# Plain and seven-product column pairs by block, and operand sums made in the output projection

## Chip, core and metric

One core of one Trainium2 chip runs one program. The time is the device time in microseconds (us); the kernel before was timed in three runs. The engines are named as in the profile: PE (TensorE, matmuls), DVE (VectorE), ACT (ScalarE), POOL (GpSimd), SP (the queue that starts most transfers). The metric is the time of the whole program, in which three feed-forward layers are the parts that the change touches.

## What is computed

Two transformer blocks over 512 tokens of width 1024, in float32. The parts around the change are three gated feed-forward layers, two in the first block (one at its start, one at its end) and one in the second:

```python
def swiglu(h, w1, w3, w2):
    return (jax.nn.silu(h @ w1) * (h @ w3)) @ w2

# first block, D_FF = 2816
x = x + 0.5 * swiglu(rms_norm(x, norm_ffn1[l]), ffn1_w1[l], ffn1_w3[l], ffn1_w2[l])
x = x + hybrid_mixer(...)
x = x + memory_attention(...)
x = x + 0.5 * swiglu(rms_norm(x, norm_ffn2[l]), ffn2_w1[l], ffn2_w3[l], ffn2_w2[l])
...
# second block, D_FF_2 = 2816
gate, up = gu[..., :D_FF_2], gu[..., D_FF_2:]
x = x + rmsnorm((jax.nn.silu(gate) * up) @ w_ffn_down[l], g_post_ffn[l])
```

Below, block 1, 2 and 3 are these three feed-forward layers in the order in which they run.

## The kernel before

Every float32 matrix is split into a high and a low part in the fast float32 form (the cast at L93 or L94 on ACT, the subtraction at L98 or L99 on DVE), and each product is three matmuls at L109: high x high, high x low, low x high. The tokens lie along the columns, 512 in all, the features along the 128 partitions.

The up stage of a feed-forward layer (`UpPairs`) makes the 22 column tiles of 128 features of both weights, "gate" and "up", in 11 pairs n = 0 to 10. A pair goes in one of two ways. A *plain* pair multiplies tile "a" and tile "b" of both weights with all 512 tokens: 2 tiles x 2 weights x 8 row tiles x 3 matmuls of 512 columns. A *seven-product* pair treats the two column tiles, the two halves of the tokens and the even and odd row tiles as 2 x 2 blocks and makes seven block products instead of eight, each of 2 weights x 4 row tiles x 3 matmuls of 256 columns. Their left operands are pieces and sums of weight tiles: f1 (products 1 and 2), s12 (6 and 5), s34 (7 and 3) and a22 (4); the sums are made on DVE at L213 and L214 (for s12) and L216 and L217 (for s34) and then split. Their right operands are pieces of x (b11 for 1, b21 for 2, b22 for 3) and sums of pieces of x (t2 for 6, t1 for 5, t3 for 7, t4 for 4). These *operand sums* are made once a layer by `Operands.sums`, for each of the four pairs of row tiles: two scaled copies on ACT (L379, L380), three small operations on DVE (L382, L383, L384), and a split (L93 on ACT, L98 on DVE). The products of a pair accumulate in three PSUM banks x, y and z; between them ACT copies bank x (L464), and DVE adds and multiplies out (L472 to L513).

`up_steps` writes the order out by hand: for a seven-product pair 1, then products 4 and 3 of the pair before it, then 2, 6, 5, 7. `PLAIN = (0, 1)` makes the first two pairs of each of the three layers plain. In block 1 `first` runs the four products of pair 0 row tile by row tile, while x comes in; in block 2 only the two of its tile "a", while the last tiles of the output projection (`out_proj` with "mo") still come out at L2041. After `first`, `sums` makes the operand sums for all four row pairs. The norm's sums over the features (8 small matmuls), the root on POOL (L325), a diagonal matrix (L332), 8 matmuls that broadcast it, and the copy to rb (L337) come behind the next plain product; outputs wait for rb. POOL squares and adds x for the norm of block 2 (L296, L300).

Weight tiles come in the order of `Stream.order`: a transfer of 512 KB into one of 6 raw buffers (L166, on SP), the weight sums two entries ahead, the split, and `next`, which works 4 entries ahead. Results of splits, operand sums, weight sums, x and the attention output all lie in one pool of 39 buffers of 4 KB a partition ("q"); temporaries lie in a pool of 8 ("b"). A planner orders each engine's instructions before the program runs; the order of the program text is its priority, and it takes later instructions forward where it expects an engine to be idle.

The functions, as they stand before:

Of the kernel before, what the change touches and what calls it, by code (L numbers as in the profile page):

```python
# [15 lines left out]
P = 128  # L16
# [3 lines left out]
KD = D // P  # L20
# [329 lines left out]
class Operands:  # L350
# [11 lines left out]
    def add(self, x1, x2, g1, g2, c=slice(0, S), pin=None):  # L362

        k = self.k
        if c.start == 0:
            self.b1.append(k.q([P, 2, S], F32R))
            self.b2.append(k.q([P, 2, S], F32R))
            self.x.append((x1, x2, g1, g2))
        j = next(j for j in range(KD // 2) if self.x[j][0] is x1)
        k.split(self.b1[j][:, 0, c], self.b1[j][:, 1, c], x1[:, c], g1, pin is not None)  # L370
        if pin is not None:
            pin()
        k.split(self.b2[j][:, 0, c], self.b2[j][:, 1, c], x2[:, c], g2, pin is not None)
# [30 lines left out]

PLAIN = (0, 1)


def up_steps():


    o, prev = [], None
    for n in range(NF // 2):
        rest = [(prev, 4), (prev, 3)] if prev is not None else []
        if n in PLAIN:
            o += [(n, "a")] + rest + [(n, "b")]
        else:
            o += [(n, 1)] + rest + [(n, 2), (n, 6), (n, 5), (n, 7)]
        prev = None if n in PLAIN else n
    return o + ([(prev, 4), (prev, 3)] if prev is not None else [])


class UpPairs:
# [8 lines left out]

    def __init__(self, k, keys, ops, finish, side=2, halves=None):
        self.k, self.keys, self.ops, self.side = k, keys, ops, side
        self.finish, self.halves = finish, halves
        self.w, self.bank, self.c = {}, {}, {}
        self.rb = None
        self.g = [k.half() if n is None else None for n in range(NF)]
# [110 lines left out]
    def run(self):  # L548
        k = self.k
        steps = up_steps()  # L550
        which = {1: "x", 6: "x", 7: "x", 4: "x", 5: "y", 3: "y", 2: "z"}
        done = {"a": "a", "b": "b", 4: "a22", 3: "s34", 5: "s12", 2: "f1"}
        last = None
        pend = []
        ps0 = self.first()
        if self.halves is None:
            self.ops.sums()
        for n, num in steps:
# [16 lines left out]
            if self.rb is None and last is not None:  # L575
                self.rb = last()
            if self.rb is not None:
                while pend:
                    m, ab, ps = pend.pop(0)
                    self.out_plain(2 * m + (ab == "b"), *ps)  # L580
                if (n, 11) in self.c:
                    z = self.c.pop((n, 11))
                    self.out(2 * n, 0, z, z)
# [74 lines left out]

def up_order(W, keys, srcs):
    seen = set()  # L660
    for n in range(NF // 2):
        W.pairs[n, keys] = {}
    for n, num in up_steps():
        what = UpPairs.LEFT[num][0]
# [1236 lines left out]
def tile_block(ctx: ExitStack, tc: tile.TileContext, aps, out):  # L1901
# [9 lines left out]
    def ffn_order(n, gate, up, down):  # L1911
        up_order(W, (gate, up), (aps[gate], aps[up]))
        for f in range(NF // 2):
# [50 lines left out]

    up = UpPairs(k, ("ffn1_w1", "ffn1_w3"), ops, lambda norm=norm: norm.finish(None, k.rb), 4)
    del ops
# [73 lines left out]
    for d, p in out_proj(k, "mo", cat, list(range(KD))):  # L2040
        nc.vector.tensor_add(x[d], p, x[d])  # L2041
        if d % 2 == 1:
            next_pair(x, ops, d - 1, G["norm_ffn2"], norm)
        nc.scalar.dma_start(x3d[d], x[d])
    x.clear()

    up = UpPairs(k, ("ffn2_w1", "ffn2_w3"), ops, lambda norm=norm: norm.finish(None, k.rb))
    del ops
# [17 lines left out]
def second_order(W, a):  # L2066
# [33 lines left out]
    for d in range(KD):  # L2100
        W.add(("wo2", d), a["w_out_2"][d])
    up_order(W, ("gate", "up"), (a["w_ffn_in"][0:NF], a["w_ffn_in"][NF : 2 * NF]))
    for f in range(NF):
# [3 lines left out]
def second_mix(k, G, x, xs, norm, norm5, k2d, v2d, dr, out):  # L2107
# [206 lines left out]

    up = UpPairs(k, ("gate", "up"), ops, finish, 6, lambda: resid(1))
    g = up.run()
# [192 lines left out]
```

## Time and profile before

| | us |
|---|---|
| median of 3 runs | 2210.93 (2210.76 to 2211.31) |
| the profiled execution | 2209.04 |
| its span, from the first to the last instruction | 2207.2 |
| PE busy | 2182.1 (99%) |
| DVE busy | 1518.6 (69%) |
| ACT busy | 1021.0 (46%) |
| POOL busy | 299.0 (14%) |

Times in the rows are from the start of the span. The up stage of block 1 lies at about 6 to 239 us, the output projection ahead of block 2 at about 765 to 804, block 2's up stage at 804 to 1033, and block 3's at 1847 to 2075. A timeline row merges neighbouring instructions of one line; the number behind x is their count, and the bracket names the idle time before them and what ended it. A matmul is drawn longer than its distance to the next one, because matmuls overlap, so the distance is read from a row's length and its count. The share of busy time over the whole span hides stages in which another engine is full; the tables by stage show those.

### The profile page before, as it was taken

The page shows a single profiled execution, that of the slowest core. Times are in us where ns is not written, and L with a number is a line of the kernel's source. Part 1 is how long each engine was busy: PE and PEld are TensorE (multiplying, and loading weights), DVE is VectorE, ACT ScalarE, POOL GpSimd, SP SyncE. Part 2 cuts the span into 40 slices and gives each one's busy share as a digit, 9 for nine tenths or more (in the row PEclk, how much of TensorE's full clock was granted, in tenths as well). Part 3 has the DMA queues.
Part 4 walks back from the last instruction along what each step waited for, and adds up shares of the span by engine and source line. Part 5 has one row for each costly group of instructions (what it writes and reads, how often), then busy time and mean ns, then how long its engine had stood idle before and what let it go on. Part 6 is the DMA issues. An engine that isn't in the chain of part 4 may idle for free.

```text
span 2207.2 us, 32709 instructions
## 1 busy us (share of the span) xinstructions
PE 2182.1 (99%) x12746; PEld 1902.7 (86%) x12746; DVE 1518.6 (69%) x2605; ACT 1021.0 (46%) x1794; POOL 299.0 (14%) x347
## 2 busy tenths in 40 slices
PE   9999999999999999999999999999999999999998
PEld 8999888878888889999888878887787789999987
DVE  7988644656866667888455955736888757888842
ACT  6554523445344544455333543315666636554620
POOL 0000021301234030000140000312334200000000
PEclk9999999999999999999999999999999999999999
DMA  5233524212333332335234123541111353133431
GB/s 177 98 114 115 177 63 136 82 58 86 122 127 105 108 112 77 115 108 178 62 114 152 54 86 101 176 148 59 41 66 53 125 177 115 58 115 106 162 106 39
DMA packets 79652, 235.73 MB, mean 107 GB/s; under 512 B 9092, under 2 KB 13444, under 8 KB 79496
## 3 DMA queue, kind: packets, MB, share of 16 engines
q1 hardware_dynamic: 75032, 226.12, 31.2%
q10 hardware_dynamic: 4464, 7.52, 0.9%
q8 instruction: 100, 1.64, 0.3%
q14 instruction: 56, 0.46, 0.1%
HBM read 216.30 MB, written 17.30 MB: 106 GB/s over the span
## 4 chain that ended last, share of the span: by engine, by line
PE 84%; DVE 8%; ACT 3%; issue 2%; POOL 2%; DMA 1%; SPq 0%; POOLq 0%; DVEq 0%; ACTq 0%
PE ps L109 82%; PE ps L118 2%; DVE q L98 2%; ACT q L93 1%; ACT q L1770 1%; DVE nx L1768 1%; POOL hr L325 1%; DVE q L99 0%; DMA raw<-in_ffn_w_dram 0%; ACT b L285 0%; DVE q L1668 0%; DVE b L289 0%; DVE q L2260 0%; DVE q L1563 0%; POOL q L1601 0%
## 5 line engine op out<-in xcount | busy, mean ns | idle before, releaser
L109 PE MATMUL ps<-q,q 128*128 128x256 f32 (+3 forms) x11736 | 2108.8, 340 | 7.7 <-ACT b L464 3.9
L109 PEld LDWEIGHTS ps<-q,q 128*128 128x128 f32 x11736 | 1794.8, 190 | 240.3 <-issue 6.6
L98 DVE TENSOR_TENSOR q<-raw,q 128x1024 fp32r<-128x1024 f32 (+3 forms) x389 | 429.6, 1122 | 97.5 <-ACT q L93 55.5
L93 ACT CAST q<-raw 128x1024 fp32r<-128x1024 f32 (+3 forms) x389 | 351.0, 931 | 106.9 <-PE ps L109 69.4
L98 DVE TENSOR_TENSOR q<-q,q 128x1024 fp32r<-128x1024 f32 (+1 forms) x188 | 189.7, 1026 | 59.3 <-ACT q L93 51.9
L93 ACT CAST q<-q 128x1024 fp32r<-128x1024 f32 (+1 forms) x188 | 164.6, 893 | 135.5 <-PE ps L109 66.0
L296 POOL TENSOR_TENSOR b<-q 128x512 f32<-128x512 f32 x32 | 36.9, 1156 | 708.4 <-DVE q L1975 301.5
L473 ACT ACTIVATE b<-b 128x256 f32<-128x256 f32 x108 | 44.9, 417 | 138.8 <-DVE b L472 138.8
L1770 ACT ACTIVATE q<-ps,nx 128x128 f32<-128x128 f32 (+3 forms) x128 | 67.4, 531 | 56.7 <-DVE nx L1768 25.8
L1775 POOL TENSOR_SCALAR q<-q,nr 128x128 f32<-128x128 f32 (+3 forms) x128 | 72.1, 569 | 143.5 <-DVE nr L1773 99.7
L118 PE MATMUL ps<-ident,q 128*128 128x128 f32 x512 | 81.3, 274 | 6.2 <-POOL q L1775 2.5
L464 ACT COPY b<-ps 128x512 f32<-128x512 f32 x81 | 47.3, 584 | 83.7 <-PE ps L109 83.7
L118 PEld LDWEIGHTS ps<-ident,q 128*128 128x128 f32 x512 | 61.8, 140 | 24.3 <-POOL q L1775 8.1
L98 DVE TENSOR_TENSOR q<-ps,q 128x512 fp32r<-128x512 f32 x112 | 74.2, 682 | 11.2 <-ACT q L93 10.8
L94 ACT ACTIVATE q<-q,gains 128x512 fp32r<-128x512 f32 (+1 forms) x48 | 30.5, 648 | 105.2 <-DVE q L1975 34.6
L300 POOL TENSOR_TENSOR b<-b,b 128x512 f32<-128x512 f32 (+1 forms) x49 | 70.4, 1444 | 2.8
L93 ACT CAST q<-ps 128x512 fp32r<-128x512 f32 x112 | 62.7, 593 | 16.8 <-PE ps L109 11.7
L1768 DVE TENSOR_REDUCE nx<-ps 128x1 f32<-128x384 f32 (+3 forms) x96 | 56.0, 584 | 0.0
L99 DVE SCALAR_TENSOR_TENSOR q<-q,gains,q 128x512 fp32r<-128x512 f32 (+1 forms) x48 | 35.6, 754 | 19.9 <-ACT q L94 19.1
L325 POOL TENSOR_TENSOR sr<-ss,mhalf 128x4 f32<-128x4 f32 x8 | 8.1, 1008 | 296.5 <-DVE ss L1400 187.3
L474 DVE TENSOR_TENSOR q<-b,b 128x256 f32<-128x256 f32 x81 | 33.8, 421 | 19.2 <-ACT b L473 18.9
L325 POOL TENSOR_TENSOR or<-ov,mhalf 128x1 f32<-128x1 f32 x4 | 2.2, 547 | 324.2 <-DVE ov L2360 324.2
(264 smaller groups left out, 1426.2 us busy)
## 6 DMA issues: line engine op xcount, KB each, us to landing
raw<-in_ffn_w_dram SPq DMA_DIRECT2D x100, 512.0 KB, 4.3
raw<-in_w_ffn_in_dram SPq DMA_DIRECT2D x44, 512.0 KB, 3.7
raw<-in_w_gm_dram SPq DMA_DIRECT2D x24, 512.0 KB, 3.3
raw<-in_ffn_w2a_dram SPq DMA_DIRECT2D x22, 512.0 KB, 4.5
raw<-in_w_ffn_down_dram SPq DMA_DIRECT2D x22, 512.0 KB, 4.4
raw<-in_w_out_dram SPq DMA_DIRECT2D x16, 512.0 KB, 3.3
raw<-in_w_mk_dram SPq DMA_DIRECT2D x8, 512.0 KB, 3.6
raw<-in_w_mv_dram SPq DMA_DIRECT2D x8, 512.0 KB, 4.0
```

Of the source, the lines that this page charges most:

```text
L93: return self.nc.scalar.copy(out, in_)
L98: return self.nc.vector.tensor_sub(out, in_, hi.bitcast(F32))
L99: return self.nc.vector.scalar_tensor_tensor(out, in_, gain, hi.bitcast(F32), op0=ALU.mult, op1=ALU.subtract)
L109: return self.nc.tensor.matmul(out, a, b, start=start, stop=stop, skip_group_check=skip)
L118: return self.nc.tensor.transpose(out, in_, self.ident[:n, :n])
L296: k.nc.gpsimd.tensor_tensor(t, x, x, op=ALU.mult)
L300: k.nc.gpsimd.tensor_tensor(self.acc, self.acc, t, op=ALU.add)
L464: self.k.nc.scalar.copy(z, bank)
L473: nc.scalar.activation(t, t, AF.Silu)
L1768: nc.vector.tensor_reduce(mx, s.rearrange("p j b t -> p b j t"), axis=AX.XY, op=ALU.max, negate=True)
L1770: nc.scalar.activation(pr[b][:, :n], s[:, :, c, :], AF.Exp, bias=mx[:, c : c + 1], accum_out=sm[:, c : c + 1])
L1775: nc.gpsimd.tensor_scalar(pr[b][:, :n], pr[b][:, :n], r[:, c : c + 1], 1.0, op0=ALU.mult, op1=ALU.mult)
```

## The change

`PLAIN` goes; the plain pairs become an argument: pair 0 alone in block 1, none in block 2, pairs 0 and 1 in block 3 as before. In block 1, pair 1 is made by seven products; the norm's sums now follow its product 1. In block 2, where no pair is plain, products 1 and 2 of pair 0 run together, row pair by row pair, in place of the plain products of tile "a", and the norm's sums follow them. The operand sums of block 2 are made in the loop of the output projection, for each row pair as soon as its two tiles of x are there, ahead of the transfer of x to x3d; the index in `Operands.add` is adapted to that, since `sums` empties its list.

```diff
@@ -366,7 +366,7 @@
-        j = next(j for j in range(KD // 2) if self.x[j][0] is x1)
+        j = next(j for j in range(len(self.x)) if self.x[j][0] is x1) + len(self.b1) - len(self.x)
@@ -402,20 +402,17 @@
         return self.th[j][:, i], self.tl[j][:, i]
 
 
-PLAIN = (0, 1)
-
-
-def up_steps():
+def up_steps(plain):
 
 
     o, prev = [], None
     for n in range(NF // 2):
         rest = [(prev, 4), (prev, 3)] if prev is not None else []
-        if n in PLAIN:
+        if n in plain:
             o += [(n, "a")] + rest + [(n, "b")]
         else:
             o += [(n, 1)] + rest + [(n, 2), (n, 6), (n, 5), (n, 7)]
-        prev = None if n in PLAIN else n
+        prev = None if n in plain else n
     return o + ([(prev, 4), (prev, 3)] if prev is not None else [])
@@ -429,8 +426,8 @@
     LEFT = {"a": ("a", 0), "b": ("b", 0), 1: ("f1", 0), 2: ("f1", 1), 3: ("s34", 1), 4: ("a22", 0), 5: ("s12", 0), 6: ("s12", 1), 7: ("s34", 0)}
     RIGHT = {1: "b11", 2: "b21", 3: "b22", 4: "t4", 5: "t1", 6: "t2", 7: "t3"}
 
-    def __init__(self, k, keys, ops, finish, side=2, halves=None):
-        self.k, self.keys, self.ops, self.side = k, keys, ops, side
+    def __init__(self, k, keys, ops, finish, plain, side=2, halves=None):
+        self.k, self.keys, self.ops, self.first_plain, self.side = k, keys, ops, plain, side
         self.finish, self.halves = finish, halves
         self.w, self.bank, self.c = {}, {}, {}
         self.rb = None
@@ -547,14 +544,28 @@
 
     def run(self):
         k = self.k
-        steps = up_steps()
+        steps = up_steps(self.first_plain)
         which = {1: "x", 6: "x", 7: "x", 4: "x", 5: "y", 3: "y", 2: "z"}
         done = {"a": "a", "b": "b", 4: "a22", 3: "s34", 5: "s12", 2: "f1"}
         last = None
         pend = []
-        ps0 = self.first()
-        if self.halves is None:
-            self.ops.sums()
+        if 0 in self.first_plain:
+            ps0 = self.first()
+            if self.halves is None:
+                self.ops.sums()
+        else:
+            ps0 = []
+
+            for w in "xz":
+                self.bank[0, w] = k.ps([P, 2, 256])
+            for j in range(KD // 2):
+                self.product(0, 1, self.bank[0, "x"], True, [j])
+                self.product(0, 2, self.bank[0, "z"], True, [j])
+            self.take(0, 1)
+            self.take(0, 2)
+            last = self.finish()
+            steps = steps[2:]
+            self.w.pop((0, "f1"))
         for n, num in steps:
             if ps0:
                 ps, ps0 = ps0[:2], ps0[2:]
@@ -574,6 +585,8 @@
                 self.take(n, num)
             if self.rb is None and last is not None:
                 self.rb = last()
+            if self.rb is None and num == 1:
+                last = self.finish()
             if self.rb is not None:
                 while pend:
                     m, ab, ps = pend.pop(0)
@@ -656,11 +669,11 @@
     return fill
 
 
-def up_order(W, keys, srcs):
+def up_order(W, keys, srcs, plain):
     seen = set()
     for n in range(NF // 2):
         W.pairs[n, keys] = {}
-    for n, num in up_steps():
+    for n, num in up_steps(plain):
         what = UpPairs.LEFT[num][0]
         if (n, what) in seen:
             continue
@@ -1909,7 +1922,7 @@
     nc.gpsimd.memset(k.mhalf, -0.5)
 
     def ffn_order(n, gate, up, down):
-        up_order(W, (gate, up), (aps[gate], aps[up]))
+        up_order(W, (gate, up), (aps[gate], aps[up]), (0,) if n == 0 else ())
         for f in range(NF // 2):
             W.add((down, "a", f), aps[down + "a"][f])
         for d in range(4, KD):
@@ -1962,7 +1975,7 @@
         norm.add_fast(x[d], True)
     x.clear()
 
-    up = UpPairs(k, ("ffn1_w1", "ffn1_w3"), ops, lambda norm=norm: norm.finish(None, k.rb), 4)
+    up = UpPairs(k, ("ffn1_w1", "ffn1_w3"), ops, lambda norm=norm: norm.finish(None, k.rb), (0,), 4)
     del ops
     g = up.run()
     for d in range(KD):
@@ -2041,10 +2054,11 @@
         nc.vector.tensor_add(x[d], p, x[d])
         if d % 2 == 1:
             next_pair(x, ops, d - 1, G["norm_ffn2"], norm)
+            ops.sums()
         nc.scalar.dma_start(x3d[d], x[d])
     x.clear()
 
-    up = UpPairs(k, ("ffn2_w1", "ffn2_w3"), ops, lambda norm=norm: norm.finish(None, k.rb))
+    up = UpPairs(k, ("ffn2_w1", "ffn2_w3"), ops, lambda norm=norm: norm.finish(None, k.rb), ())
     del ops
     g = up.run()
     for d in range(KD):
@@ -2099,7 +2113,7 @@
         W.add(("proj", 0, d), a["w_proj_nsa"][d])
     for d in range(KD):
         W.add(("wo2", d), a["w_out_2"][d])
-    up_order(W, ("gate", "up"), (a["w_ffn_in"][0:NF], a["w_ffn_in"][NF : 2 * NF]))
+    up_order(W, ("gate", "up"), (a["w_ffn_in"][0:NF], a["w_ffn_in"][NF : 2 * NF]), (0, 1))
     for f in range(NF):
         W.add(("down", f), a["w_ffn_down"][f])
@@ -2312,7 +2326,7 @@
 
         return second
 
-    up = UpPairs(k, ("gate", "up"), ops, finish, 6, lambda: resid(1))
+    up = UpPairs(k, ("gate", "up"), ops, finish, (0, 1), 6, lambda: resid(1))
     g = up.run()
     gb = k.q([P, 2, S])
     nc.sync.dma_start(gb, k.a["g_post_rows"])
```

## Rows read from the trace of the kernel before

**Rows 1.** The page: header, PE, granted clock by slices, the chain that ended last:

```profile
span 2207.2 us, 32709 instructions
...
PE 2182.1 (99%) x12746; PEld 1902.7 (86%) x12746; DVE 1518.6 (69%) x2605; ACT 1021.0 (46%) x1794; POOL 299.0 (14%) x347
...
PEclk9999999999999999999999999999999999999999
...
PE 84%; DVE 8%; ACT 3%; issue 2%; POOL 2%; DMA 1%; SPq 0%; POOLq 0%; DVEq 0%; ACTq 0%
```

**Rows 2.** The table by stage for L109: window, PE busy (count), weight loads, granted clock, DMA:

```profile
core 0: us, PE busy (x) PEld busy (x), PEclk, DMA share, GB/s
70.00:110.00 40.00, 40.00 (x335) 40.00 (x335) 1.00 0.33 107
...
190.00:230.00 40.00, 40.00 (x335) 40.00 (x335) 1.00 0.39 122
...
245.00:280.00 35.00, 35.00 (x156) 28.99 (x155) 1.00 0.44 138
```

**Rows 3.** The timeline of PE at the start of block 1: start, length, engine, line, operation:

```profile
6.37 6.64 PE L109 MATMUL ps<-q,q 128*128 128x512 f32 x25
...
13.30 21.84 PE L109 MATMUL ps<-q,q 128*128 128x512 f32 x95 [0.29 <-DVE q L99]
...
34.97 0.95 PE L109 MATMUL ps<-ones,b 128*128 128x1 f32 x8
...
42.18 22.68 PE L109 MATMUL ps<-q,q 128*128 128x512 f32 x144
...
66.72 43.45 PE L109 MATMUL ps<-q,q 128*128 128x256 f32 x360 [1.86 <-ACT b L464]
```

**Rows 4.** The timeline of DVE there: weight splits, operand sums, then a weight sum:

```profile
24.35 1.22 DVE L98 TENSOR_TENSOR q<-raw,q 128x1024 fp32r<-128x1024 f32 x1
...
29.65 0.42 DVE L382 TENSOR_TENSOR q<-b,b 128x256 f32<-128x256 f32 x1
...
30.56 0.69 DVE L384 TENSOR_TENSOR q<-b,q 128x512 f32<-128x512 f32 x1
...
32.52 1.23 DVE L98 TENSOR_TENSOR q<-q,q 128x1024 fp32r<-128x1024 f32 x1 [1.27 <-ACT q L93]
...
45.03 1.23 DVE L98 TENSOR_TENSOR q<-q,q 128x1024 fp32r<-128x1024 f32 x1 [1.11 <-ACT q L93]
...
46.18 0.68 DVE L213 TENSOR_TENSOR q<-raw 128x512 f32<-128x512 f32 x1
```

**Rows 5.** The timeline of ACT there: an operand sum's cast, then a weight tile's:

```profile
43.96 1.05 ACT L93 CAST q<-q 128x1024 fp32r<-128x1024 f32 x1 [3.75 <-DVE q L384]
44.91 1.05 ACT L93 CAST q<-raw 128x1024 fp32r<-128x1024 f32 x1
```

**Rows 6.** The timeline of SP there: transfers of weight tiles issued:

```profile
17.28 3.41 SPq L166 DMA_DIRECT2D raw<-in_ffn_w_dram  x4
```

**Rows 7.** Tables by stage over all engines: late in block 1, then block 2's output projection:

```profile
core 0: us, PE busy (x) PEld busy (x) DVE busy (x) ACT busy (x) POOL busy (x), PEclk, DMA share, GB/s
190.00:230.00 40.00, 40.00 (x335) 40.00 (x335) 34.28 (x53) 20.24 (x30) 0.00 (x0) 1.00 0.39 122
...
772.00:804.00 32.00, 32.00 (x143) 26.50 (x142) 19.35 (x19) 10.33 (x13) 16.92 (x13) 1.00 0.48 156
```

**Rows 8.** Timelines at the start of block 2: DVE, POOL and ACT:

```profile
803.92 0.69 DVE L2041 TENSOR_TENSOR q<-ps,q 128x512 f32<-128x512 f32 x1 [2.63 <-PE ps L109]
...
805.40 0.93 DVE L99 SCALAR_TENSOR_TENSOR q<-q,gains,q 128x512 fp32r<-128x512 f32 x1 [0.79 <-ACT q L94]
...
805.87 1.62 POOL L300 TENSOR_TENSOR b<-b,b 128x512 f32<-128x512 f32 x1
...
825.13 1.99 ACT L93 CAST q<-raw 128x1024 fp32r<-128x1024 f32 x2
```

## The prediction

> **What bounds the kernel now.** I read the page first. TensorE (PE) is busy for 2182 of 2207 us at full clock, and 84% of the chain that ended last is PE [rows 1]: the time falls only where PE gets less to do, and rises by every us for which PE has to wait. The next view is the table by stage for the matmul line, since the change swaps one kind of product for another. In a stage of seven-product pairs 335 matmuls of 256 columns go in 40.00 us, 119.4 ns each; in a stage of 512 columns 156 go in 35.00 us, 224 ns [rows 2]. Some records may be missing from such a count, so I check it on the first plain pair: 95 matmuls in 21.84 us less the 0.2 us by which the last is drawn out, 228 ns [rows 3]. I take 226 ns. Last come the timelines around the places that change, to see what lies beside PE there: VectorE (DVE) [rows 4], ScalarE (ACT) [rows 5], the transfer queue [rows 6], and DVE's load by stage [rows 7]; for the second block [rows 8].
>
> **The change part by part.** *The matmuls.* A plain pair is 2 tiles x 2 weights x 8 x 3 = 96 matmuls of 512 columns: 96 x 226 ns = 21.7 us. A seven-product pair is 7 x 2 x 4 x 3 = 168 of 256 columns: 168 x 119.4 ns = 20.0 us. Three pairs change kind, so PE loses 3 x 1.7 = 5.1 us of work: 1.7 in block 1, 3.4 in block 2. The transfers stay: four weight tiles for a pair of either kind. The Trainium skill (TensorE: Matmul & The Clock Gate, section "Back-to-back issue gap") gives 2.5 ns over the columns at 2.4 GHz for each matmul, so 109 and 216 ns, a gain of 2.4 us a pair; the measured spacings differ from it, and with its figures the whole sum below would be 2.1 us lower.
>
> *The work beside PE.* A seven-product pair costs DVE 34.28/2 = 17.1 us of each 20 [rows 7]; a plain one costs four splits and four output steps, about 4 x 1.14 + 4 x 0.60 = 7 us by their spacing. So a plain pair is also a cover: 14 us in which DVE can do other things. That is what is taken away.
>
> *Block 1.* Before, PE has issued 25 + 95 = 120 matmuls when the norm sums start at 34.97 us, 24 of them of the second plain pair [rows 3]; pair 0 therefore ends at 34.97 - 24 x 0.226 = 29.5 us. At 29.65 DVE starts the operand sums and ends them at 45.03 + 1.23 = 46.2 us: four steps of 3.9 us, each three small operations, a cast on ACT, and a subtraction that waits for the cast [rows 4]. All that is hidden behind the second plain pair; t2 is wanted first by product 6 of pair 2, after 53 us. Now pair 1 has seven products. Products 1 and 2 (48 matmuls, 5.7 us) need no sums; the norm sums take some 0.8 us of the 0.95 that are drawn, and the broadcast, eight small matmuls too, as much [rows 3]. At 29.5 + 7.3 = 36.8 us product 6 wants t2, and nine matmuls later, at 37.9, its last quarter. Even if the operand sums ended at 46.2 as before, PE would wait.
>
> They end later. In the text the splits of f1 and s12 and the weight sums for s12 and s34 stand ahead of the operand sums. The four splits replace the four of the plain pair; the weight sums are new: 8 operations of 0.68 us, spaced by 0.60 [rows 4], 4.9 us. Could DVE do them in the gaps between the steps? All these results lie in the pool of 39 q buffers, and the trace says that its buffers are given out in the order of the text: the transfers of pair 2's f1 tiles were issued by 20.7 us [rows 6], ACT sat idle for 3.75 us ahead of 43.96, and yet their cast begins at 44.91, behind the last cast of the operand sums, after which it stands in the text [rows 5]. Block 2 shows the same at 825.13 [rows 8]. So I put the 4.9 us ahead of the chain: the sums end at about 51.1 us.
>
> In the meantime PE can do the three quarters of products 6 and 5 whose operands are there, 36 matmuls or 4.3 us if it may run ahead within a bank, 2.1 us if not. The wait is 51.1 - 36.8 - 4.3 = 10.0 us, at most 12.2; with the sums at 46.2 it would be 5.1. Behind product 6 on PE stand products 5 and 7 and the next pair's first; nothing else of the kernel can run there. The splits for product 7 follow the sums on DVE (2.3 us) while PE still has 12 matmuls (1.4 us) and the first half of product 7 needs one split only: 0.2 us more. Against that, the 1.86 us for which PE waited at 66.72 behind a copy on ACT [rows 3] belongs to the old change from plain to seven-product pairs and goes. Block 1: 10.2 - 1.7 - 1.9 = +6.6 us (bounds +1.5 and +8.8).
>
> *Block 2.* The output projection has room: 19.35 of 32.00 us busy on DVE [rows 7], 12.6 free, against three chains of 2.8 us of DVE work and four weight sums (2.4) before the last x. The fourth chain decides. x7 is added at 803.92, its split ends at 806.33 [rows 8]; 1.5 + 1.05 + 1.23 us of sums follow: 810.2. PE starts on products 1 and 2 at 803.9, is through at 809.6, does the norm sums (0.8), and comes to the last quarter of t2 at 811.5. The norm's accumulator is ready at 805.87 + 1.62 = 807.5 on POOL [rows 8], 2 us before PE asks. Before, the cover was two plain pairs; now it is 1.3 us, and each us of DVE work that slips ahead of the fourth chain beyond that is a us of wait. Two splits of s12 may (2.3 us): I set 0.2 us, with bounds 0 and 3.5. The x3d transfers, now behind the sums in ACT's text, cost nothing: they are read again only in the next stage. Block 2: -3.4 + 0.2 = -3.2 us.
>
> Sum: +6.6 - 3.2 = +3.4 us. On the profiled execution (2209.04 us, span 2207.2) that is 2212.4; the median lies 1.89 us above it, so 2214.3 us.
>
> **The rivals.** *A, the forecast* (0.47): as above, 2212.5 to 2217. *B, the wait also costs clock* (0.15, slower): PE never waits longer than 1.9 us today and the granted clock is full throughout [rows 1, 3], so no row shows what a wait of 10 us, in pieces of 3 to 4, does. Were it to fall to 1.2 GHz, the remaining 12 matmuls and the 24 of product 7 would take twice 119 ns: +4.3 us, 2218.6. The Trainium skill (same page, section "HAM oscillation — how this bites in real kernels") says that PE's clock is halved after idle gaps and comes back with activity; no run here shows it yet. *C, block 2 loses its gain* (0.12, slower): near 803 us the q pool would hold x 1, the attention output 8, b 8, t 6, two output weights 4, f1 4, s12 4 and weight sums 4, which is 39, all there are; if s12 and s34 have to wait for the projection's end, their 4.6 us of splits and sums come ahead of the fourth chain, which takes the 3.4 us: 2217.7. It decides from 1.3 us of slip. *D, the gaps are filled* (0.16): if the weight sums go into the 1.1 us in which DVE waits for each cast, the operand sums end at 46.4 and the wait is 5.3: block 1 +1.9, sum -1.3, 2209.6. For it speaks that DVE is idle there; against it rows 4 to 6. *E, all is hidden* (0.10, faster): the planner puts the operand sums ahead of all else and PE waits no longer than the 1.9 us of today: -5.1, 2205.8. The sums would have to be ready by 38 us, 8 earlier than now, with DVE busy without a gap from 24.35 [rows 4].
>
> **How the numbers follow.** The likeliest is A: 2214.3. A measurement can tell about 0.2%, 4.4 us: 2206.5 and 2215.4 are the limits. Faster is E: 0.10. Slower is B, C and the upper fifth of A: 0.15 + 0.12 + 0.10 = 0.37. The rest of A and D is the same: 0.53. The range leaves out E and the far ends of B and C: 2208.5 to 2219.
>
> **What would show it.** In the profile after: PE spacing unchanged; in block 1 an idle PE between 37 and 51 us put down to the subtraction or cast of the operand sums; weight sums ahead of them on DVE; the last sum at about 51 us; a granted clock below 1.00 there if B holds; in block 2 no PE wait over 1 us and the up stage some 3 us shorter. Wrong would be: operand sums in block 1 done by 40 us, or a PE wait around 810.

## The result and the profile after

The kernel after the change takes 2228.81 us (median, 2228.33 to 2229.81), the kernel before, on the same chip, 2211.11: a ratio of 1.0082, 95% interval [1.0071, 1.0093], slower by 17.7 us where +3.4 was forecast. The range ended at 2219.0.

To place the time I use landmarks that both kernels have. Block 2's first addition of a projection output to x (L2041 before, L2054 after) starts at 770.60 us before and at 782.34 after: +11.7, all of block 1. The first matmul of the down projection behind block 2 starts at 1033.05 before and at 1052.44 after: from landmark to landmark 262.45 and 270.10, so block 2 gives +7.7. That sums to 19.4; the two spans (2207.2 and 2226.5) differ by 19.3, so block 3 adds nothing. The medians differ by 1.7 less, because the trace before is of a quick run (2209.04, median 2211.11): twelve traces of this study have block 1 as before, and their first x addition starts at 770.53 to 773.60. So block 1's share is uncertain by some 3 us. Block 2's is firm: four traces with its two plain pairs give 262.45 or 262.46 us.

The page of the kernel after (header, busy time by engine, granted clock by slices), which answers to [rows 1]:

```profile
span 2226.5 us, 33227 instructions
...
PE 2186.7 (98%) x12962; PEld 1916.9 (86%) x12962; DVE 1553.2 (70%) x2662; ACT 1036.5 (47%) x1821; POOL 300.0 (13%) x347
...
PEclk8999999999999999999999999999999999999999
```

PE has less to do (three times 168 matmuls of 256 columns in place of 96 of 512), and yet its busy time has risen by 4.6 us: part of its matmuls ran slower. The first slice of the clock, now 8, says where to look. The timeline of PE at the start of block 1 (start, length, engine, line, operation, count, idle time before and what ended it), for [rows 3]:

```profile
32.63 0.95 PE L109 MATMUL ps<-ones,b 128*128 128x1 f32 x8
33.45 3.11 PE L109 MATMUL ps<-q,q 128*128 128x256 f32 x24
41.95 2.36 PE L109 MATMUL ps<-b,ones 128*128 128x128 f32 x8 [5.39 <-DVE b L332]
43.96 2.74 PE L109 MATMUL ps<-q,q 128*128 128x256 f32 x12
48.38 0.50 PE L109 MATMUL ps<-q,q 128*128 128x256 f32 x2 [1.68 <-ACT q L93]
49.64 1.13 PE L109 MATMUL ps<-q,q 128*128 128x256 f32 x4 [0.76 <-DVE q L98]
52.23 0.80 PE L109 MATMUL ps<-q,q 128*128 128x256 f32 x2 [1.47 <-ACT q L93]
53.49 81.77 PE L109 MATMUL ps<-q,q 128*128 128x256 f32 x668 [0.47 <-DVE q L98]
```

Five waits, 9.77 us in all, in the place that was forecast. But the longest, 5.39 us, is for the norm's diagonal matrix (L332), not for an operand sum. The timeline of DVE there, for [rows 4]:

```profile
35.87 0.42 DVE L382 TENSOR_TENSOR q<-b,b 128x256 f32<-128x256 f32 x1
...
40.07 0.15 DVE L317 TENSOR_SCALAR nv<-ps 128x4 f32<-128x4 f32 x1
...
41.52 0.28 DVE L332 TENSOR_SCALAR b<-ident,nr 128x128 f32<-128x128 f32 x1 [0.91 <-POOL nr L325]
...
52.22 3.50 DVE L98 TENSOR_TENSOR q<-q,q 128x1024 fp32r<-128x1024 f32 x3 [1.11 <-ACT q L93]
```

The norm's sums leave PE at 33.6, but L317, which reads them, comes only at 40.07: on DVE it stands behind weight sums, splits and the first operand sums. The root on POOL and L332 follow, and 1.9 us after L317's start PE goes on. The operand sums begin at 35.87, behind the weight sums, as forecast; the last one's split ends at 52.22 + 3.50/3 = 53.4, not at 51.1. The granted clock by stage (window, PE busy with its count, clock, DMA):

```profile
35.00:40.00 5.00, 1.56 (x14) 0.95 0.33 120
40.00:45.00 5.00, 3.05 (x13) 0.50 0.00 0
45.00:50.00 5.00, 2.57 (x13) 0.84 0.00 0
50.00:55.00 5.00, 3.07 (x13) 0.50 0.02 3
55.00:60.00 5.00, 5.00 (x38) 0.84 0.00 0
60.00:65.00 5.00, 5.00 (x44) 1.00 0.16 40
```

Behind the first wait the clock falls to the lower level, 1.2 GHz, and is back for good only after 55 us. (In the trace before it was 1.00 in every stage read, [rows 2].) In block 2 PE looks like this, then the clock by stage:

```profile
825.61 2.88 PE L109 MATMUL ps<-q,q 128*128 128x256 f32 x11 [5.56 <-DVE q L99]
828.29 1.77 PE L109 MATMUL ps<-ones,b 128*128 128x1 f32 x8
829.91 5.29 PE L109 MATMUL ps<-q,q 128*128 128x256 f32 x24
835.88 1.32 PE L109 MATMUL ps<-q,q 128*128 128x256 f32 x9 [0.68 <-ACT b L461]
```

```profile
816.00:820.00 4.00, 4.00 (x34) 1.00 0.17 66
820.00:825.60 5.60, 0.05 (x1) 0.91 0.52 171
825.60:828.00 2.40, 2.39 (x10) 0.50 0.38 147
828.00:830.00 2.00, 2.00 (x12) 0.50 0.00 0
830.00:835.00 5.00, 5.00 (x25) 0.52 0.00 0
835.00:840.00 5.00, 4.33 (x37) 1.00 0.01 3
```

PE waits 5.56 us, not for an operand sum but for the split of x7 itself (L99), the last of x's eight tiles, and then runs some 9 us at half clock. DVE had not come to x7. Its timeline, and POOL's:

```profile
806.76 1.77 DVE L213 TENSOR_TENSOR q<-raw 128x512 f32<-128x512 f32 x1
...
813.14 1.39 DVE L382 TENSOR_TENSOR q<-b,b 128x256 f32<-128x256 f32 x1
...
818.44 1.78 DVE L216 TENSOR_TENSOR q<-raw,raw 128x512 f32<-128x512 f32 x1
...
824.22 0.68 DVE L2054 TENSOR_TENSOR q<-ps,q 128x512 f32<-128x512 f32 x1
```

```profile
805.83 2.15 POOL L300 TENSOR_TENSOR b<-b,b 128x512 f32<-128x512 f32 x1
...
812.63 1.61 POOL L300 TENSOR_TENSOR b<-b,b 128x512 f32<-128x512 f32 x1
...
817.51 2.16 POOL L300 TENSOR_TENSOR b<-b,b 128x512 f32<-128x512 f32 x1
```

x7's addition (L2054) starts at 824.22, 41.9 us behind the first one; before it was 33.3 (803.92, [rows 8]). The three long DVE rows took 0.69, 0.42 and 0.69 us elsewhere. Each starts while POOL is in an addition (L300) and ends 0.29 to 0.55 us after that ends.

### The profile page after: what moved, and what is told of

It reads as the page before. It is cut to its first block, busy times and chain, and to the rows that moved or that the text cites. A ratio compares the mean times of both kernels' runs of the same rounds, so it can differ in the third digit from the quotient of the medians.

```text
span 2226.5 us, 33227 instructions
## 1 busy us (share of the span) xinstructions
PE 2186.7 (98%) x12962; PEld 1916.9 (86%) x12962; DVE 1553.2 (70%) x2662; ACT 1036.5 (47%) x1821; POOL 300.0 (13%) x347
## 4 chain that ended last, share of the span: by engine, by line
PE 84%; DVE 8%; issue 3%; ACT 3%; POOL 1%; DMA 1%; SPq 0%; ACTq 0%; DVEq 0%; POOLq 0%
PE ps L109 81%; PE ps L118 2%; DVE q L98 2%; ACT q L1783 1%; DVE q L99 1%; DVE nx L1781 1%; ACT q L93 1%; POOL hr L325 1%; DVE b L289 0%; DMA q<-in_cmp_w_v_dram 0%; DMA raw<-in_ffn_w_dram 0%; DVE q L2274 0%; SPq L250 0%; DVE q L1576 0%; DMA q<-in_xT_dram 0%
## 5 line engine op out<-in xcount | busy, mean ns | idle before, releaser
L109 PE MATMUL ps<-q,q 128*128 128x256 f32 (+4 forms) x11952 | 2111.8, 337 | 17.1 <-DVE q L99 6.0
L109 PEld LDWEIGHTS ps<-q,q 128*128 128x128 f32 x11952 | 1808.2, 191 | 239.9 <-DVE q L99 7.5
L98 DVE TENSOR_TENSOR q<-raw,q 128x1024 fp32r<-128x1024 f32 (+3 forms) x389 | 428.0, 1116 | 102.3 <-ACT q L93 60.6
L93 ACT CAST q<-raw 128x1024 fp32r<-128x1024 f32 (+3 forms) x389 | 348.3, 925 | 109.0 <-PE ps L109 76.2
L98 DVE TENSOR_TENSOR q<-q,q 128x1024 fp32r<-128x1024 f32 (+1 forms) x200 | 204.5, 1045 | 57.3 <-ACT q L93 50.0
L93 ACT CAST q<-q 128x1024 fp32r<-128x1024 f32 (+1 forms) x200 | 176.1, 902 | 123.4 <-PE ps L109 66.4
L470 ACT ACTIVATE b<-b 128x256 f32<-128x256 f32 x120 | 49.9, 417 | 142.4 <-DVE b L469 142.2
L461 ACT COPY b<-ps 128x512 f32<-128x512 f32 x90 | 52.6, 584 | 100.9 <-PE ps L109 100.6
L98 DVE TENSOR_TENSOR q<-ps,q 128x512 fp32r<-128x512 f32 x112 | 74.2, 683 | 11.1 <-ACT q L93 10.7
L300 POOL TENSOR_TENSOR b<-b,b 128x512 f32<-128x512 f32 (+1 forms) x49 | 71.5, 1464 | 2.8
L93 ACT CAST q<-ps 128x512 fp32r<-128x512 f32 x112 | 62.7, 592 | 16.8 <-PE ps L109 11.6
L99 DVE SCALAR_TENSOR_TENSOR q<-q,gains,q 128x512 fp32r<-128x512 f32 (+1 forms) x48 | 36.4, 769 | 15.4 <-ACT q L94 14.9
```

The source lines that it names most:

```text
L93: return self.nc.scalar.copy(out, in_)
L98: return self.nc.vector.tensor_sub(out, in_, hi.bitcast(F32))
L99: return self.nc.vector.scalar_tensor_tensor(out, in_, gain, hi.bitcast(F32), op0=ALU.mult, op1=ALU.subtract)
L109: return self.nc.tensor.matmul(out, a, b, start=start, stop=stop, skip_group_check=skip)
L300: k.nc.gpsimd.tensor_tensor(self.acc, self.acc, t, op=ALU.add)
L461: self.k.nc.scalar.copy(z, bank)
```

## Experiments

Each ratio below is to the kernel before on the same chip. "Block 2" in us is from its first x addition to the down projection, as above.

**One block at a time.** Block 1's change alone and block 2's change alone:

```diff
 # block 1 alone: block 2 plain again, its sums in run()
-(0,) if n == 0 else ()
+(0,) if n == 0 else (0, 1)
 # block 2 alone
-(0,) if n == 0 else ()
+(0, 1) if n == 0 else ()
```

> The change in block 1 alone; block 2 as before (two plain pairs, operand sums behind them). Theory (the two blocks lose independently; block 1 loses its cover for the operand sums and the matrix clock falls in the wait): +11.7 us, 2222.8 us, which is the shift of block 2's start between the two traces. Rival (block 1's shift is repaid or enlarged by what follows in block 2): away from +11.7 by more than 1 us.

> The change in block 2 alone; block 1 as before. Theory (x7's addition and split queue on VectorE behind weight sums and splits, PE waits 5.6 us for them, the clock falls): +7.6 us, 2218.7 us, the rest of the difference between the traces. Rival (block 2 suffers from block 1's delay, by transfers or buffers): below +5 us.

Block 1 alone: 2221.67 us, ratio 1.0051 [1.0036, 1.0066], +10.9. Block 2 alone: 2218.44, 1.0034 [1.0021, 1.0047], +7.7. They add up to 18.6, about the 17.7 of both. So the two misses are independent and can be studied apart.

**Block 2: moving the sums, and one pair fewer.** The sums made in the projection with two plain pairs kept, then with one; block 1 as before in both (the matching argument in `ffn_order` is not shown):

```diff
-    up = UpPairs(k, ("ffn2_w1", "ffn2_w3"), ..., ())
+    up = UpPairs(k, ("ffn2_w1", "ffn2_w3"), ..., (0, 1))   # or (0,)
```

> Both blocks keep two plain pairs; only the operand sums of block 2 are made in the loop of the output projection. Theory (the move itself costs nothing, since the plain products need no sums and their rows of x come in as before): 0 us, within 0.5, no PE wait over 0.7 us in block 2. Rival (the sums in the projection hold up x7 on VectorE by themselves): a PE wait of 4 us or more near the end of the projection, +4 to +8 us.

> Block 1 as before; block 2 with pair 0 plain, pair 1 by seven products, and the operand sums in the output projection. Theory (one plain pair is cover enough for the last operand sums and the first weight sums): -1.7 us, one pair's difference of PE work, 2209.4 us. Rival (the projection's end is overloaded on VectorE whatever follows): 0 to +6 us.

The move alone: 2210.54, ratio 1.0000 [0.9991, 1.0010]. With one plain pair left: 2209.77, 0.9996 [0.9986, 1.0005]; block 2 takes 261.69 us, 0.8 under before, with one PE wait of 0.6 us. So neither the move nor the first pair costs anything; the loss comes with the last cover.

**Is it POOL that holds DVE?** Block 2's change alone, with the squares and additions on POOL left out for seven of the eight x tiles (so the norm there sums one tile only):

```diff
-    if pin is None:
+    if pin is None and norm.first:
         norm.add(x[d])
-        norm.add(x[d + 1])
```

> The change in block 2 alone, with the squares and additions of GpSimd for the norm left out for seven of the eight tiles of x (so block 2's norm is that of one tile). Theory A (VectorE operations with two SBUF inputs stand still while GpSimd runs: 0.4 to 1.1 us each, 4.4 us between x4 and x7): those operations take 0.4 to 0.7 us instead of 1.1 to 1.8, x7's addition comes 4 us earlier, PE waits 1 to 2 us instead of 5.6, the clock stays up, 2211 to 2213. Theory B (only the order of the text on VectorE matters, s34 ahead of x7): PE's wait stays above 4.5 us and the time above 2217.

2210.02 us, ratio 0.9994 [0.9985, 1.0004]: 8.4 us under the same kernel with them, though no DVE instruction was taken away, and only x6's addition changed places. PE and DVE there:

```profile
811.59 0.95 PE L109 MATMUL ps<-ones,b 128*128 128x1 f32 x8
812.40 1.43 PE L109 MATMUL ps<-q,q 128*128 128x256 f32 x10
814.34 1.94 PE L109 MATMUL ps<-q,q 128*128 128x256 f32 x14 [0.51 <-DVE q L98]
816.95 1.33 PE L109 MATMUL ps<-q,q 128*128 128x256 f32 x9 [0.68 <-ACT b L461]
```

```profile
806.56 1.28 DVE L2053 TENSOR_TENSOR q<-ps,q 128x512 f32<-128x512 f32 x2
...
810.33 0.43 DVE L382 TENSOR_TENSOR q<-b,b 128x256 f32<-128x256 f32 x1 [0.43 <-ACT b L380]
```

The wait for L99 is gone, L382 is back at 0.43, and x6 and x7 are added one behind the other at 806.56 (L2053 is that line here), 34 us behind the first, 7.4 us earlier for x7 where theory A had 4. The clock stays at 1.00. Block 2 takes 260.81 us, 1.64 under before.

As a sum this also shows what the half clock took. Block 2 is 270.11 us with POOL's work and 260.81 without, 9.30 apart. PE's waits there are 5.56 + 0.68 = 6.24 and 0.51 + 0.68 = 1.19, 5.05 apart. The other 4.25 us have no wait to go with; they fit the stretch at half clock, in which 35 products and the norm's sums, 35 x 0.119 + 0.8 = 5.0 us of work, took 9.6. Not all of it could be won back: at full clock PE would have come about 1.3 us ahead of the last operand sum's split (an estimate: 816.24 + 5.0 against 822.6 in block 2's change alone).

**The same without leaving anything out.** Squares on ACT, additions on DVE:

```diff
-        norm.add(x[d])
-        norm.add(x[d + 1])
+        norm.add_fast(x[d])
+        norm.add_fast(x[d + 1])
```

> Block 2's change alone, with the norm's squares of the eight x tiles on ScalarE and their sums on VectorE in place of GpSimd; all of the computation is there. Theory (GpSimd holds VectorE's instructions with two SBUF inputs): the L382 and L216 instructions of the projection last 0.42 and 0.69 us everywhere, the PE wait for L99 (5.56 us) falls below 2 us, the clock stays at 1.00, and the time is 2208 to 2213 us, near the 2210.0 without the squares, although VectorE now has seven additions of about 0.69 us (4.8 us) more. Rival (VectorE has just too much to do there, whoever does the squares): the seven additions put x7's split off as far as GpSimd did, the wait stays at 3 to 6 us, the time at 2215 to 2219.

> Block 1 as before; block 2 with pair 0 plain, the operand sums in the projection, and the norm's squares on ScalarE and VectorE. If the GpSimd hold also costs this version, it gains on the 2209.8 of the same without that change: 2207.5 to 2209.5, below the kernel before by 0.1%. Rival: with a plain pair as cover there was no PE wait left to gain (0.6 us in all), so it stays at 2209.5 to 2211, or loses up to 1 us by the seven additions.

With no plain pair: 2213.88, ratio 1.0014 [1.0005, 1.0023], a little above the range that was expected; 4.6 us better than with POOL in spite of seven more DVE instructions. With one plain pair: 2208.71, 0.9990 [0.9982, 0.9999], the fastest kernel of this study, 2.0 us under the kernel before; against the same kernel with POOL's work (0.9996) the gain lies inside the two intervals. No PE wait is left at the start of block 2, and it takes 260.81 us, 1.64 under before: the 1.7 of one pair, and all of it. PE in the first of the two, and its clock:

```profile
815.73 0.38 PE L109 MATMUL ps<-q,q 128*128 128x256 f32 x1 [1.25 <-ACT q L93]
816.99 3.36 PE L109 MATMUL ps<-q,q 128*128 128x256 f32 x14 [0.88 <-DVE q L98]
821.02 2.29 PE L109 MATMUL ps<-q,q 128*128 128x256 f32 x9 [0.68 <-ACT b L461]
```

```profile
812.00:816.00 4.00, 2.75 (x23) 2.45 (x21) 2.69 (x7) 2.00 (x4) 1.12 (x1) 1.00 0.02 4
816.00:820.00 4.00, 3.12 (x15) 3.01 (x14) 4.00 (x4) 2.52 (x3) 0.00 (x0) 0.50 0.00 0
820.00:825.00 5.00, 4.33 (x20) 4.03 (x20) 2.35 (x6) 1.53 (x2) 0.00 (x0) 0.50 0.00 0
```

The long wait is gone, and the forecast's own picture appears: short waits for the fourth chain's cast and subtraction, 2.1 us (a further 0.29 stood ahead of them). But the clock (the number before the last two) falls all the same. Block 2 takes 267.11, +4.7: -3.4 of matmuls, +3.1 of waits, and 5.0 that goes with the half clock. This trace is of the slowest of the kernel's ten runs: 2215.91 us with a mean granted clock of 0.996. The two quickest took 2211.63 and 2211.68 us at 0.999 and 0.998, and all ten are in order: the lower the clock, the longer the time. So 5.0 us is the dear end of what the clock costs here, and the median, 2213.88 against 2210.68 for the kernel before on that chip, is the price of having no cover with POOL out of the way.

**The order of the text in block 2.** Weight splits held back until the projection is out:

```diff
         nc.scalar.dma_start(x3d[d], x[d])
+        if d == 5:
+            W.AHEAD = 2
+    W.AHEAD = Stream.AHEAD
```

> The change in block 2 alone, with the weight stream held back at the end of the output projection (two entries ahead instead of four after d = 5), so that the splits of s12 and the sums and splits of s34 stand behind x6 and x7 in the text. Theory B (q buffers go out in the order of the text, so these stood ahead of x6's and x7's splits): x7's addition follows the projection's last matmul within 1.5 us, the wait for L99 is gone; a new wait of 1 to 3 us comes at product 6, for s12 or the last operand sums; 2211 to 2214. Theory A alone (GpSimd's hold on VectorE): PE still waits 4 us or more for L99, 2217 or more.

2217.92, ratio 1.0033 [1.0021, 1.0045]: x7's addition came at 809.84 as expected, and the waits moved on, 2.33 us for a cast (L93) and 1.37 for a subtraction (L98), with half clock. The wait for L99 fell to 0.23 and 0.58 us, as theory B had it, but the time missed its 2211 to 2214: DVE has the same work to do ahead of product 6, in whichever order.

**Block 1 without its operand sums.** Products 4 to 7 read pieces of x instead, so that part of the computation is left out:

```diff
-                self.ops.sums()
+                self.ops.th, self.ops.tl = [[b.rearrange(...) for b in self.ops.b1]] * 2
```

> Block 1's change alone, without the operand sums of block 1: products 4 to 7 read pieces of x instead, so this part of the computation is left out, with the same matmuls. Theory (the wait for the sums, and the half clock that follows it, are all of the loss): no PE wait over 1 us between 30 and 70 us, clock 1.00, and the time falls below the kernel before by the matmuls' 1.7 and the old 1.9 us stall: 2206 to 2209 us against 2221.7 with the sums. Rival (the weight splits and weight sums of pair 1 don't keep up with seven-product pairs from the start, sums or not): PE waits of 3 us or more on casts and subtractions of weight tiles stay, half clock too, and the time is 2212 to 2218.

2210.43, ratio 1.0000 [0.9991, 1.0009]. Without the sums the +10.9 of block 1 is gone; but the time does not fall below the kernel before, as my theory had it. PE there, then a row of the table by stage:

```profile
40.01 1.25 PE L109 MATMUL ps<-b,ones 128*128 128x128 f32 x8 [3.38 <-DVE b L332]
40.92 49.36 PE L109 MATMUL ps<-q,q 128*128 128x256 f32 x397
```

```profile
40.00:45.00 5.00, 4.99 (x30) 5.00 (x30) 3.81 (x9) 3.33 (x5) 0.00 (x0) 0.66 0.02 3
```

The wait for the norm's diagonal matrix stays, 3.38 us, with a clock of 0.66 from 40 to 45 us, where 30 matmuls went in place of the 44 that five us hold at full clock (1.7 us). -1.7 - 1.9 + 3.4 + 1.7 = +1.5; the down projection behind block 1 starts at 240.79, against 239.21 before: +1.6. That agreement proves little, because the twelve traces with block 1 as before start it at 239.08 to 242.65, and by the medians the two kernels are equal. What is shown is the wait: the norm's way over DVE, POOL and DVE is a second loss of block 1, which the prediction did not have.

**The order in block 1.** Only f1's split ahead of the operand sums, the weight sums behind them:

```diff
+                k.W.AHEAD, k.W.SUMS = 2, 0
             ps0 = self.first()
             if self.halves is None:
                 self.ops.sums()
```

> The change in block 1 alone, with only f1 split ahead of the operand sums (two entries ahead and no weight sums ahead, until the operand sums are in the text). Theory (the 8 weight sums and 2 splits ahead of the operand sums cost what they take): the operand sums end near 46 us instead of 53.5, product 6 then waits for s12 until about 48 to 50, and the time is 3 to 6 us below that of block 1 alone, 2216 to 2219. Rival (the chain of the operand sums starts no earlier, for lack of x or ScalarE): within 1 us of 2221.7.

2220.42, ratio 1.0040 [1.0026, 1.0054], 1.3 us below block 1 alone and inside its interval, where 3 to 6 were expected. The operand sums did end earlier, at 45.5 in place of 53.6, so the weight sums and two splits ahead of them cost what the prediction said, and more. But the wait for L332 stayed at 3.17 us, and then PE waited 6.80 us for a cast (L93) of the weight sums for s12, which now came behind. It ran on without a wait from 50.31 in place of 53.7, at a clock of 0.50 up to 55 us, and of these 3.4 us little reaches the time.

**Fillers against the clock.** Small matmuls of ones in PE's waits. First in block 1, 24 behind product 2 and 24 behind product 5; then in block 2, 44 ahead of the last row pair of products 1 and 2:

```diff
                 self.take(n, num)
+                if self.first_plain == (0,) and n == 1 and num in (2, 5):
+                    k.warm(24)
 # block 2
+                if j == 3:
+                    k.warm(44)
```

> The change in block 1 alone, with 48 matmuls on constants that go nowhere behind products 2 and 5 of pair 1, where PE waits. Theory (the wait costs twice, once as idle time and once because the clock then stands at 1.2 GHz for the matmuls behind it): the granted clock stays at 1.00 through 60 us and the time falls below that of the change in block 1 alone (2221.7) by 1.6 to 4.3 us, to 2217.4 to 2220.1. Rival (the sums on VectorE set the pace whatever the clock): within 0.7 us of 2221.7, or above it by the filler's own time.

> Block 2's change alone, with 44 small matmuls (ones by ones, 128 columns) put into the place on PE where it waits 5.56 us for x7's split, ahead of the last row pair of products 1 and 2; at the 0.115 us that such matmuls take at full clock that is 5.1 us, a little under the wait. Block 2's change alone took 2218.4 us, with half clock for some 9 us behind the wait. Theory (about half of the loss in block 2 is clock, and it falls because PE stands idle): the clock stays near 1.00 from 816 to 840 us, the 9 us at half clock give back about 4 us, and the time is 2213 to 2215.5. Rival 1 (all of the loss is the wait and the traffic on VectorE; the lower clock stretches only matmuls that would wait anyway): 2217.5 to 2219. Rival 2 (the fillers end after x7's split, or run at half clock themselves): 2219 to 2223, with the fillers' row ending behind the split.

Both slower than without fillers: 2225.21, 1.0064 [1.0049, 1.0079], and 2223.05, 1.0056 [1.0039, 1.0072]. Each such matmul makes two rows of the trace, so the fillers were twice as long as I had meant (88 rows, 9.98 us, in block 2), and the copy of product 1 (L461) fell behind five casts on ACT, a new wait of 3.14 us. Inconclusive on the price; but while they ran the clock stayed at 1.00, and in block 2 it fell to 0.50 behind the 3.14. Then with 20 fillers of 8 columns, which leave the order of all other work as it was, in block 2's wait and in block 1's:

```diff
+                    k.warm(20, 8)   # ones[:, 0:8] as the moving side
```

> Block 2's change alone with 20 small matmuls (ones by ones, 8 columns; 40 rows of the trace, some 0.115 us each as the 128-column and 1-column ones have it, 4.6 us) put on PE into the 5.56 us wait for x7's split; the order of everything else on every engine stays that of block 2's change alone (2218.4 us). Theory (the half clock of some 9 us behind the wait is on the path): with PE kept busy the clock stays at 1.00 from 816 to 825; PE is then through the norm's sums and 24 products at about 821.2 and waits for the last operand sum's split (822.6), in place of arriving at 825.8: up to 3.2 us come back, 2215 to 2216.5. Rival 1 (the clock costs nothing, the sums set the pace anyway): 1.00 in the rows, but 2217.5 to 2219. Rival 2 (so narrow matmuls don't hold the clock, or something else lowers it): 0.50 stays behind the wait, 2217.5 to 2219.

> Block 1's change alone with the same 20 small matmuls of 8 columns in its 5.39 us wait for the norm's diagonal matrix (L332), everything else in the order of block 1's change alone (2221.7 us). Theory: until the last operand sum is split at about 53.5 us the clock costs nothing here, since PE waits for the sums anyway; what the clock costs is the stretch behind it, 156 matmuls in 21.44 us in place of 18.6, 2.8 us. If the clock stays up through the later waits of 1 to 2 us, the time is 2218.5 to 2220; if those waits lower it again, 2221 to 2222.5. Rival (the half clock of 40 to 50 us is on the path too): 2215 to 2218.

2218.52, 1.0036 [1.0022, 1.0050], and 2221.22, 1.0047 [1.0032, 1.0062]: nothing gained. PE and its clock in block 2:

```profile
809.81 4.53 PE L109 MATMUL ps<-ones 128*128 128x8 f32 x40
...
815.65 2.88 PE L109 MATMUL ps<-q,q 128*128 128x256 f32 x11 [1.09 <-DVE q L99]
```

```profile
816.00:820.00 4.00, 4.00 (x20) 3.91 (x19) 3.93 (x5) 1.78 (x4) 2.10 (x2) 0.50 0.16 61
```

PE counts as busy through the wait but for 1.09 us, and the clock behind it is 0.50 just as without the fillers (rival 2). In block 1 the same fillers left no wait for L332 at all, and the clock from 40 to 45 us was still 0.50. Last, a pair with and without 20 fillers of 128 columns, in which the order could be kept by making the fourth sums behind the copy of product 1:

```diff
             self.take(0, 1)
+            self.ops.sums()
             self.take(0, 2)
 # second of the pair, ahead of j == 3
+                    k.warm(20)
```

> Block 2's change alone, with the operand sums of the fourth row pair made behind the copy of product 1 (the other three stay in the projection). It is the partner of the next run, which adds fillers to it. PE's wait for x7's split (5.6 us) and the half clock behind it stay; the fourth sums come about 0.6 us later by the copy: 2217.5 to 2220.

> The run before this with 20 small matmuls of 128 columns (40 rows, 4.6 us) in PE's wait for x7's split; the order of all other work on all engines stays, but for one pair of neighbours on VectorE. Theory (the half clock behind the wait is on the path): clock 1.00 through 815 to 825 us, and the time 1.5 to 4 us below the run before. Rival (the clock costs nothing, VectorE's chain behind x7 sets the pace): clock 1.00, but PE waits for the fourth sums instead, and the time is within 1 us of the run before.

2222.97, 1.0054 [1.0039, 1.0069], and 2223.38, 1.0051 [1.0034, 1.0068]. The first missed its band: the later fourth sums brought waits of 1.42 and 0.68 us of their own. With the fillers the first wait is 1.10, but others follow (0.47, 1.49, 0.68), and the clock is 0.68 from 816 to 820 and 0.50 to 0.55 on to 835, where without fillers it was back by 830. So the price of the clock was not isolated by fillers: what kept it up was having no longer waits than 0.51 and 0.68 us (the run without POOL's work).

## Why the prediction was wrong, step by step

*The matmuls* (-1.7 a pair): right. One pair fewer and no wait gave -1.64.

*Block 1, the wait* (+10.2): nearly the right sum, of the wrong parts. 9.77 us were measured, and part of the nearness is luck: the half clock stretched PE's work between the waits by some 3.9 us (the 5.9 less the 2.0 below), and at full clock these would have been waiting too. The step that failed is the norm at "some 0.8 us" and the broadcast "as much": those are PE's own times. Between them lies the way over L317, POOL and L332, which the second plain pair had covered, and I named no cover for it. It is the 5.39 us wait, and 3.38 even with the sums gone. The way itself takes only 1.9 us; the other 6.5 us from the norm's sums on, L317 stood in its place on DVE, and no run put it ahead of the other work there. Second, the sums' end at 51.1: 53.4 was measured. The order (weight sums and splits first) was as forecast (behind the operand sums they let these end at 45.5), but I left out what products 1 and 2 and the norm put on DVE between the four chains: L317, L332, L498, L481 twice and L469, from 0.15 to 0.95 us each. The old 1.9 us stall went, as forecast.

*Rival B* (0.15) was the case in block 1. From 41.95 to 135.26 us PE had 688 products and the broadcast, 688 x 0.1194 + 0.9 = 83.1 us of work, and 4.38 of waits; it took 93.3: 5.9 us for the clock, where B had 4.3. 9.8 + 5.9 - 1.7 - 1.9 = 12.1, against 11.7 by the landmark. Not all of the 5.9 lies on the path, since PE waited for the sums until 53.5 anyway; what lies behind that, 81.77 us for 668 products in place of 79.8, is 2.0. The error was the choice: the rows could not show what a long wait does to the clock, and I gave the costless end 0.47 and this one 0.15. Later traces show that even the old stall can bring the clock down: nine of the twelve with block 1 as before have a fall behind it, and the one that I had read is among the three without. The Trainium skill (TensorE: Matmul & The Clock Gate, section "HAM oscillation — how this bites in real kernels") says that PE's clock is halved after idle gaps; the trace agrees, 0.50 behind the 5.39 and the 5.56 us. It belonged in the likeliest case.

*Block 2* (-3.2, measured +7.7): the step that failed is "The output projection has room", with "12.6 free". The 12.6 us are free only if DVE's instructions keep their lengths. In that window POOL was busy for 16.92 us [rows 7], and DVE's instructions with two operands in SBUF were held while it worked. The kernel before shows it; I had not read the row. Two weight splits there, the first of them while POOL adds:

```profile
784.11 1.63 POOL L300 TENSOR_TENSOR b<-b,b 128x512 f32<-128x512 f32 x1
...
784.65 3.30 DVE L98 TENSOR_TENSOR q<-raw,q 128x1024 fp32r<-128x1024 f32 x2
```

Two splits take 2.35 elsewhere. With the sums and weight sums moved in, more such instructions met POOL, and x7's addition slipped from 33.3 us behind the first to 41.9; without POOL it came at about 34. So the forecast's end of x7's split, 806.33, lay 9 us early. The Trainium skill (SBUF — State Buffer, section "Who interferes with whom") says just this: a VectorE instruction with two SBUF inputs contends with a GpSimd instruction that reads SBUF, and whoever comes second blocks fully. L382 at 1.39 in place of 0.42 agrees. I also put the wait at the last quarter of t2; it came earlier, at products 1 and 2. The sum by rows: -3.4 + 6.24 of waits + 4.6 of clock = +7.4.

*Rival C* had the direction for block 2 and, in part, the mechanism (weight work ahead of the fourth chain stood there), but not the size: it took only the gain away, and x7 itself was late. D and E fell: the sums did not fill gaps, and PE waited. (E's "busy without a gap from 24.35" misreads [rows 4], whose brackets show DVE idle for 1.27 and 1.11 us within the operand sums.)

What stays open: how the clock's share divides between "on the path" and "beside another wait" in block 1, what decides whether a wait of 1 to 2.4 us lowers the clock, and what block 1 would take with the norm's instructions put first on DVE.

## What to carry to other kernels

A stage that feeds a slower path is not only work, it is cover: before it is taken away, list every round trip that runs beside it (here the norm's way over three engines, the operand sums, and the weight work), and not only the one that the change is about. Free time of VectorE was free here only outside the time in which GpSimd worked on SBUF tiles; count POOL's busy time against it, and try the work on ScalarE and VectorE where the window is tight. When TensorE is at 99%, a new wait of a few us may cost up to about twice its length (4.6 us of half clock behind 5.56 and 0.68 of waits in block 2), since the matmuls behind it may run at half clock; the version with one pair as cover and no wait kept its whole gain. And a single trace shows the clock of one run: read it in several before calling it full.

## What the runs showed of the hardware

- A DVE instruction with two SBUF operands that starts while POOL adds is held until POOL's instruction ends: L382 1.39 us in place of 0.42, L216 1.78 in place of 0.69. POOL is held too: its additions took 2.15 and 2.16 us where a split (L98) was under way at their start, and 1.60 to 1.62 where none was. Leaving out 14 of POOL's instructions brought x7 forward by 7.4 us with no DVE instruction less.
- Short waits can halve the clock too: 1.25 and 0.88 us, one after the other, were followed by 9 us at 0.50 and cost 5.0 us beyond the waits. The same wait does so in one run and not in another: in the twelve traces with block 1 as before, the clock fell behind the stall at about 66 us in nine (waits of 2.32 to 2.35 us; 0.50 to 0.70 in the lowest stretch of 2 or 5 us) and not in three (1.86 us in [rows 3], 2.07 and 2.34 us). Its length alone does not decide it.
- Forty rows of 8-column matmuls in a wait left the clock behind it at 0.50, in block 1 with the whole wait filled; 88 rows of 128 columns held it at 1.00 while they ran.
